# A three-branch encoder layer on one core: operands of the merge stored as parts by the stages that make them, the merge's sums on VectorE, and its weights split one token group earlier

## The chip, the core and the metric

The kernel runs on one core of a Trainium2 chip. The metric is the device time of one execution in microseconds (us). Three executions of the kernel before took 2923.69, 2925.81 and 2926.0 us; the median is 2925.81. The core has five engines with one instruction stream each: TensorE (PE in the profile; its weight loads are PEld), VectorE (DVE), ScalarE (ACT), GpSimd (POOL) and SyncE (SP). Here SP issues every DMA. A stream is worked in order, so an instruction that waits holds up all that stands behind it on its engine.

## What is computed

One layer over 2048 prompt tokens and 8 samples of 16 tokens (17 tiles of 128 tokens), model width 1024:

```python
h = rms_norm(x, norm_g[l])
(a_x, a_b, a_c, a_z, g_q, g_f, g_i, g_z, s_q, s_k, s_v, s_z, m_a, m_b, m_c) = split_cols(h @ w_in[l])
o_a = a_b * causal_conv(a_c * a_x) * silu(a_z)             # A: gated convolution
o_b = rms_norm(hgrn_scan(g_q, g_f, g_i)) * silu(g_z)       # B: gated linear recurrence
o_c = stick_breaking_attention(s_q, s_k, s_v) * silu(s_z)  # C: attention
y_a, y_b, y_c = o_a @ wb[:512], o_b @ wb[512:1024], o_c @ wb[1024:]
m = sigmoid(m_a) * y_a + sigmoid(m_b) * y_b + sigmoid(m_c) * y_c
out = x + m @ w_out[l]
```

## The kernel before, in words

**Parts.** A float32 product is made of three products of shorter floats: each operand is split into a high part (ACT casts it) and a low part (DVE subtracts the high part from the source), and high·high, low·high and high·low are summed (`PASS3`). `split` (L172) issues the two instructions.

**Stages.** (1) Three token groups (5, 6 and 6 tiles, two chunks each; `run_jobs`, L1241). A job is one weight block of `w_in`: 128 columns for channel jobs (24 matmuls of 384 tokens a chunk, L683) or 256 for token jobs (L694). In group 0 `wload` (L180) loads a block into a staging tile `wst` (2 buffers), splits it into a tile `w` (3 buffers, 1 MB, both parts), and `wkeep` (L204) stores the parts in DRAM; groups 1 and 2 load the kept parts straight into a `w` tile. A job's weights are loaded one job ahead. (2) The merge (L1308 to L1438): four groups of token tiles; for each, 12 branch jobs (L1368; 4 for each branch x) and 4 output jobs (L1403), the output jobs of a group between the branch jobs of the next. The merge's own weights (12 blocks of `w_branch`, 8 of `w_out`) are split and kept in the first merge group.

**Background.** Generators of other work are advanced by a budget while the main loop is traced: the recurrence, the attention of the samples (traced during group 1), the prompt's attention (during group 2 and the merge). The final order on each engine is made by a scheduler from the order of tracing and the readiness of operands and buffers, so it moves when tiles or waits change.

**Operands of the merge.** The branches store their results to `OX` in float32 (conv L917, recurrence L1092, attention L344, samples L530). `load_o` (L1329) loads four slices of a branch into `ost` (2 buffers), multiplies those of the attention by the gate `SZ` (L1338), and splits them into `oh` and `ol`. A branch job multiplies its product by the gate `GM` on DVE (L1374, L1376); the sum over branches is a POOL instruction (L1377) except in the last group's last branch; after the third branch the sum `mp` is split into `mh` and `ml`, by a list `due` that holds a split back by one token chunk or two.

**Attention.** For each block of keys: scores into `z` (L306, L307), two sigmoids on ACT (`snb` L310, `sp` L312), a scan and a product on DVE (L319, L324), transposes on PE (L291), a copy of them to `aT` on ACT (L292), and the product with the values (L336). `aT` is one buffer.

Of the kernel before, what the change touches and what calls it, by code (L numbers as in the profile page):

```python
# [16 lines left out]
P = 128  # L17
# [81 lines left out]
def trunk(ctx: ExitStack, tc: tile.TileContext, x_prompt, x_sample, cache_conv, state_hgrn, cache_k, cache_v,  # L99
# [55 lines left out]
    OX = dram.tile([3, 4, P, NTOK], F32, name="OX")  # L155
# [20 lines left out]


    kept = {}

    def wload(pieces, key, places=None):  # L180
# [3 lines left out]
        for n, v in enumerate(pieces):  # L184
            a, b = v.shape[1], v.shape[2]
            w = places[n] if places else wp.tile([P, 2, 1024], F32R, tag="w", name="w")
# [17 lines left out]
    def wkeep(out, key):  # L204
        for n, (_, _, w) in enumerate(out):
# [72 lines left out]
    def attn_pair(m0, m1):  # L278
# [14 lines left out]

        for m in range(m0, m1):
            _, _, si, last, b0, b1, e = steps[m]
            load_step(m)
            load_step(m + 1)
            Q1, Q2, Kt, Vt = held[m]
# [66 lines left out]
    def sample_attention():  # L365
# [163 lines left out]
        nc.scalar.copy(ot, tp.rearrange("p (j t) -> p j t", j=4))  # L529
        nc.sync.dma_start(OX[2][:, :, S0].rearrange("j p t -> p j t"), ot)  # L530
# [26 lines left out]
    class Prepare:  # L557
# [35 lines left out]
        def turn(self, i, kk):  # L593
            ci, ti, _ = self.tiles[i]
            if ti == 0 and kk == 0:
                hh = hp.tile([P, KB, 384], F32R, tag="hh", name="hh")
                hl = hp.tile([P, KB, 384], F32R, tag="hl", name="hl")
                self.hT[ci] = (hh, hl, len(self.group[ci]) * P)
# [242 lines left out]
    class Conv:  # L841
# [67 lines left out]
        def az(self, ci, acc):  # L909
# [7 lines left out]
            nc.sync.dma_start(OX[0, self.j][:, cols(chunk)], y)  # L917
# [39 lines left out]
    def recurrence(g, h, f, k, q, gz, v):  # L957
# [4 lines left out]
        for unit in units:  # L962
# [129 lines left out]
            nc.sync.dma_start(OX[1, h][:, (first + unit[0]) * P:(first + unit[0]) * P + n], ob[:, :n])  # L1092
            yield 0.5

# [145 lines left out]

    def run_jobs(g, jobs):  # L1241
# [5 lines left out]
        def weights(i):  # L1247
            if i < n and i not in ws:
# [5 lines left out]
                 + [(n - 2, 0), (n - 1, 0), (n - 2, 1), (n - 1, 1)])  # L1254
        for at_, (i, ci) in enumerate(order):
            weights(i)
# [52 lines left out]
    wb = w_branch[0]  # L1309
    wo = w_out[0]  # L1310
    GMAX = max(sum(len(c) for c in pg) for pg in PGROUPS) * P

    def branch_w(x, dp):
        return ([wb[x * 512:(x + 1) * 512, dp * 256:(dp + 1) * 256].rearrange("(k p) m -> p k m", p=P)],
                ("branch", x, dp))

    def out_w(s):
        v = wo[:, s * 256:(s + 1) * 256].rearrange("(k p) m -> p k m", p=P)
# [149 lines left out]
```

## Time and profile before

| | |
|---|---|
| median of three runs | 2925.81 us |
| the profiled execution | 2919.97 us, span 2918.1 us |
| PE busy | 2873.3 us (98%) |
| DVE, ACT, POOL busy | 1530.7, 1024.7, 427.9 us |
| moved by DMA | 597.82 MB, mean 205 GB/s |

Busy time is time in which an engine executes; its idle time is put down to what released it at last. The span begins with the first instruction and ends with the last. In the profile of before the first token group ends near 600 us, the second near 1346 us and the third near 2184 us; the merge takes the rest. "PEclk" is the granted share of TensorE's 2.4 GHz.

### The profile page before, as it was taken

How to read it: one execution, taken by the hardware profiler on the slowest of the kernel's cores; microseconds unless marked ns; L12 is line 12 of the kernel's file. 1: busy time of each engine (PE TensorE's matmuls, PEld its weight loads, DVE VectorE, ACT ScalarE, POOL GpSimd, SP SyncE). 2: the span in 40 equal slices, each digit the busy share in tenths (PEclk: the TensorE clock that was granted, in tenths of full speed). 3: DMA queues.
4: the chain of work that ended last, by engine and by line, in shares of the span. 5: the costliest groups of instructions: out<-in, count | busy, mean ns of one | idle time of the engine just before them, and what ended most of it. 6: DMA issues, size and time to landing. Idle time of an engine off the chain costs nothing.

```text
span 2918.1 us, 51343 instructions
## 1 busy us (share of the span) xinstructions
PE 2873.3 (98%) x19511; PEld 2672.2 (92%) x19511; DVE 1530.7 (52%) x3182; ACT 1024.7 (35%) x2359; POOL 427.9 (15%) x859
## 2 busy tenths in 40 slices
PE   9999999999999999999999999999999899999999
PEld 9999999999999999999999999999988787687888
DVE  5454644641252423345434747265577876867643
ACT  4333223242222222114333443334444554444420
POOL 3200000120100000002231111101012412313210
PEclk9999999999999999999999999999999999999999
DMA  8977677767556564436764444434347776677666
GB/s 305 315 257 236 223 227 237 239 229 250 182 184 204 168 213 147 150 128 195 237 200 154 140 151 134 152 121 150 126 155 252 258 268 219 224 251 227 222 230 233
DMA packets 329224, 597.82 MB, mean 205 GB/s; under 512 B 29097, under 2 KB 231170, under 8 KB 291090
## 3 DMA queue, kind: packets, MB, share of 16 engines
q1 hardware_dynamic: 328978, 594.54, 61.8%
q8 instruction: 155, 2.54, 0.4%
q14 instruction: 91, 0.75, 0.1%
HBM read 410.62 MB, written 183.80 MB: 204 GB/s over the span
## 4 chain that ended last, share of the span: by engine, by line
PE 87%; DVE 4%; DMA 4%; issue 3%; POOL 2%; ACT 1%; SPq 0%; DVEq 0%; POOLq 0%; ACTq 0%
PE acc L683 45%; PE acc L694 13%; PE acc L1403 6%; PE acc L1368 4%; PE pv L336 4%; PE tp L291 3%; PE z L1013 2%; PE z L307 2%; PE z L306 2%; DVE pr L319 1%; PE tp L434 1%; POOL mp L1377 1%; DMA w<-W 1%; PE pv L498 1%; DMA gate<-GM 1%
## 5 line engine op out<-in xcount | busy, mean ns | idle before, releaser
L683 PE MATMUL acc<-hh,w 128*128 128x384 f32 (+1 forms) x5376 | 1465.0, 338 | 0.0
L683 PEld LDWEIGHTS acc<-hh,w 128*128 128x128 f32 x5376 | 964.3, 188 | 23.6 <-issue 17.9
L683 PE MATMUL acc<-hl,w 128*128 128x384 f32 (+1 forms) x2688 | 882.5, 328 | 0.0
L683 PEld LDWEIGHTS acc<-hl,w 128*128 128x128 f32 x2688 | 507.1, 189 | 4.9 <-issue 1.0
L694 PE MATMUL acc<-w,hh 128*128 128x256 f32 x2176 | 413.1, 286 | 1.5 <-DMA w<-W 1.2
L694 PEld LDWEIGHTS acc<-w,hh 128*128 128x128 f32 x2176 | 341.8, 188 | 4.0 <-DMA w<-W 1.5
L319 DVE TENSOR_TENSOR_SCAN pr<-snb,carry 128x513 f32<-128x513 f32 x192 | 250.6, 1306 | 117.1 <-ACT snb L310 115.6
L694 PE MATMUL acc<-w,hl 128*128 128x256 f32 x1088 | 306.8, 282 | 0.7 <-DVE hl L175 0.7
L1368 PE MATMUL acc<-oh,w 128*128 128x512 f32 (+2 forms) x960 | 295.4, 368 | 4.2 <-DMA w<-W 1.8
L292 ACT COPY aT<-tp 128x512 f32<-128x512 f32 (+2 forms) x320 | 167.6, 525 | 289.7 <-PE tp L291 289.4
L324 DVE TENSOR_TENSOR sp<-sp,pr 128x512 f32<-128x512 f32 (+2 forms) x320 | 210.3, 657 | 33.7 <-POOL sp L315 7.8
L310 ACT ACTIVATE snb<-z 128x512 f32<-128x512 f32 (+2 forms) x320 | 172.5, 539 | 129.2 <-PE z L307 120.3
L1368 PEld LDWEIGHTS acc<-oh,w 128*128 128x128 f32 x960 | 176.3, 190 | 36.9 <-DVE gate L1376 5.1
L694 PEld LDWEIGHTS acc<-w,hl 128*128 128x128 f32 x1088 | 205.1, 189 | 1.8 <-DVE hl L175 1.3
L319 DVE TENSOR_TENSOR_SCAN pr<-snb,one 128x129 f32<-128x129 f32 (+3 forms) x128 | 114.7, 896 | 163.1 <-POOL snb L315 162.9
L1403 PE MATMUL acc<-w,mh 128*128 128x256 f32 x960 | 189.1, 285 | 2.5 <-DMA w<-W 2.3
L291 PE MATMUL tp<-idf,sp 128*128 128x128 f32 x1088 | 172.0, 273 | 8.1 <-ACT aT L292 7.2
L175 DVE TENSOR_TENSOR w<-wst,w 128x1024 fp32r<-128x1024 f32 x92 | 114.9, 1249 | 121.6 <-ACT w L174 121.1
L1368 PE MATMUL acc<-ol,w 128*128 128x512 f32 (+1 forms) x480 | 174.1, 363 | 3.2 <-DVE ol L175 3.1
L312 ACT ACTIVATE sp<-z 128x512 f32<-128x512 f32 (+2 forms) x320 | 171.3, 535 | 12.6 <-DMA OX<-ot 7.5
L1403 PEld LDWEIGHTS acc<-w,mh 128*128 128x128 f32 x960 | 153.7, 188 | 10.6 <-issue 5.2
L1146 ACT ACTIVATE gm<-acc 128x384 f32<-128x384 f32 (+1 forms) x144 | 68.3, 474 | 260.8 <-PE acc L683 223.0
(296 smaller groups left out, 3730.9 us busy)
## 6 DMA issues: line engine op xcount, KB each, us to landing
w<-W SPq DMA_DIRECT2D x200, 1024.0 KB, 5.3
W<-w SPq DMA_DIRECT2D x92, 1024.0 KB, 5.0
wst<-in_w_in_dram SPq DMA_DIRECT2D x72, 512.0 KB, 6.3
GM<-gm SPq DMA_DIRECT2D x120, 192.0 KB, 2.7
Kt<-KT SPq DMA_DIRECT2D x160, 128.0 KB, 3.6
gate<-GM SPq DMA_DIRECT2D x72, 256.0 KB, 3.1
vc<-in_cache_v_dram SPq DMA_DIRECT2D x64, 256.0 KB, 3.8
kc<-in_cache_k_dram SPq DMA_DIRECT2D x64, 256.0 KB, 3.5
```

The source lines that it names most:

```text
L175: return first, (eng or nc.vector).tensor_tensor(lo, src, hi.bitcast(F32), ALU.subtract)
L291: nc.tensor.transpose(tp[:, j * P:(j + 1) * P], sp[:, j * P:(j + 1) * P], idf)
L292: nc.scalar.copy(aT[:, e, 0:nb, i * P:(i + 1) * P], tp[:, :w].rearrange("p (b q) -> p b q", q=P))
L310: nc.scalar.activation(sn[:, 512 - w:512], z[:, :w], AF.Sigmoid, scale=-0.125)
L312: nc.scalar.activation(sp[:, :w], z[:, :w], AF.Sigmoid, scale=0.125)
L319: nc.vector.tensor_tensor_scan(pr[:, 512 - w:513][:, ::-1], s_in, s_in, one if diag else carry[e][i], ALU.mult, ALU.bypass)
L324: nc.vector.tensor_tensor(sp[:, :w], sp[:, :w], pr[:, 513 - w:513], ALU.mult)
L336: nc.tensor.matmul(pv[64 * e:64 * e + 64, c0:n], Vt[:, j, e], aT[:, e, j, c0:n], start=first and j == 0, stop=last and j == nb - 1, skip_g ...
L683: nc.tensor.matmul(acc[:, :n], w[0][a][:, k], hT[b][:, k, :n], start=k == 0 and i == 0, stop=k == KB - 1 and i == 2)
L694: nc.tensor.matmul(acc[:, :256], hT[b][:, k, ti * P:(ti + 1) * P], w[k // 4][a][:, k % 4], start=k == 0 and i == 0, stop=k == KB - 1 and i ...
L1368: nc.tensor.matmul(acc[:, :n], w[0][a][:, k, dd * P:(dd + 1) * P], box[x][b][:, k, sl], start=k == 0 and i == 0, stop=k == 3 and i == 2)
L1403: nc.tensor.matmul(acc[:, :256], box["l" if b else "h"][:, k, ti * P:(ti + 1) * P], w[k // 4][a][:, k % 4], start=k == 0 and i == 0, stop= ...
```

## The change

- The three stages store both parts: `OX` has a dimension of 2, and `store_parts` splits a result where it is made and stores two tiles. The attention and the samples load `SZ` there and multiply on DVE before the split. `load_o` then only loads eight slices into one tile `o`.
- The sums `mp` are all on DVE, and their split follows at once; `due` is gone.
- The merge's weights are split and stored in group 1: at the second chunk of a channel job, after the ninth place of the order, one of 20 pieces is loaded, split and kept (`split_merge_weights`). The merge loads parts only.
- Every fourth load of kept parts goes to the two staging buffers `wst`, as two DMAs of 0.5 MB, instead of to a `w` tile. The last jobs' places in `oh` and `ol` are gone.
- `hh` and `hl` become one tile `hx` of the same size. The first branch of the next merge group is loaded at an earlier job.

```diff
+    def store_parts(dst, where, x, room):
+        split(room.bitcast(F32R), x.bitcast(F32R), x)
+        for v, part in enumerate((room, x)):
+            nc.sync.dma_start(dst[v][:, where].bitcast(F32), part)
...
+            if (key, n) in kept:
+                turns[0] += 1
+                if turns[0] % 4 == 0:
+                    hl = []
+                    for i in range(2):
+                        x = wp.tile([P, a, b], F32, tag="wst", name="wst", bufs=2)
+                        nc.sync.dma_start(x, kept[key, n][:, i].rearrange("p (a b) -> p a b", a=a).bitcast(F32))
+                        hl.append(x.bitcast(F32R))
+                    out.append((*hl, None))
+                    continue
+            w = wp.tile([P, 2, 1024], F32R, tag="w", name="w")
...
         def store():
-            t = at.tile([P, 512], F32, tag="sp", name="ot", bufs=4)
-            nc.scalar.copy(t[:, :n], box[0][:, :n])
-            nc.sync.dma_start(OX[2, pair][:, q0:q0 + n], t[:, :n])
+            t = gate[0]
+            nc.vector.tensor_tensor(t[:, :n], box[0][:, :n], t[:, :n], ALU.mult)
+            th = at.tile([P, 512], F32, tag="oth", name="oth", bufs=1)
+            store_parts(OX[2, pair], slice(q0, q0 + n), t[:, :n], th[:, :n])
...
+    def split_merge_weights():
+        for pieces, key in [branch_w(x, dp) for x in range(3) for dp in range(4)] + [out_w(s) for s in range(4)]:
+            for n, v in enumerate(pieces):
+                wkeep(wload([v], key, n), key, n)
+                yield
...
+            if ci and len(jobs[i][0][0]) == 1 and at_ > 8:
+                next(extra, None)
             weights(i)
...
-            oh = p3.tile([P, 4, GMAX], F32R, tag="oh", name="oh", bufs=2)
-            ol = p3.tile([P, 4, GMAX], F32R, tag="ol", name="ol", bufs=2)
+            o = p3.tile([P, 2, 4, GMAX], F32R, tag="o", name="o", bufs=2)
             for j in range(4):
-                st = p3.tile([P, GMAX], F32, tag="ost", name="ost", bufs=2)
-                nc.sync.dma_start(st[:, :ntok], OX[x, j][:, gcols])
...
-                split(oh[:, j, :ntok], ol[:, j, :ntok], st[:, :ntok])
+                for v in range(2):
+                    nc.sync.dma_start(o[:, v, j, :ntok].bitcast(F32), OX[x, j, v][:, gcols].bitcast(F32))
...
-                            (nc.vector if final and x == 2 else nc.gpsimd).tensor_tensor(
-                                m, m, gate[:, sl], ALU.add)
+                            nc.vector.tensor_tensor(m, m, gate[:, sl], ALU.add)
                         if x == 2:
-                            box["due"].append((box["h"][:, d, sl], box["l"][:, d, sl], m))
-                            while len(box["due"]) > (0 if final or d == 7 and chunk is pg[-1] else len(pg)):
-                                split(*box["due"].pop(0))
+                            split(box["h"][:, d, sl], box["l"][:, d, sl], m)
```

**What it moves.** First, SP in group 1, kernel before: the loads (L189) of the kept parts of three consecutive jobs (`W31`, `W32`, `W40`), among the gates' stores (GM) and the samples' keys and values (`kc`, `vc`).

```order
L189 DMA w_10549<-W31_3251 128x2048
L1147 DMA GM_77<-gm_10408 128x384
L431 DMA kc_10653<-in_cache_k_dram 128x512
L431 DMA kc_10679<-in_cache_k_dram 128x512
L1147 DMA GM_77<-gm_10481 128x384
L431 DMA kc_10813<-in_cache_k_dram 128x512
L189 DMA w_10670<-W32_3314 128x2048
```

The same place after: `wst_10814` and `wst_10921` stage two pieces of `w_out`; `W85`, `W86` are the stores of their parts; L208 loads kept parts.

```order
L211 DMA wst_10814<-in_w_out_dram 128x4x256
L211 DMA wst_10921<-in_w_out_dram 128x4x256
L529 DMA OCS_78<-od_10960 16x64
L208 DMA w_10870<-W32_3330 128x2048
L227 DMA W85_10818<-w_10813 128x2048
L227 DMA W86_10925<-w_10920 128x2048
L529 DMA OCS_78<-od_10960 16x64 x6
L1175 DMA GM_77<-gm_10989 128x384
L208 DMA w_10992<-W40_4034 128x2048
```

The load of `W32` now stands behind two staging loads, and that of `W40` behind the stores of two split pieces.

Second, PE at the same job, before: the last matmuls with the parts of `W31` (`w_10549`) and the first with those of `W32` (`w_10670`), with sample attention some matmuls earlier (L498, L452, L456).

```order
L498 MATMUL pv_10309<-vc_10715,at__10709 32x128 x4
L452 MATMUL z_10739<-kt_10652,qz_6938 32x256 x4
L456 MATMUL z_10739<-knew_6946,qz_6938 32x16 x4
L683 MATMUL acc_10720<-hh_6911,w_10549 128x384
L683 MATMUL acc_10720<-hl_6912,w_10549 128x384
L683 MATMUL acc_10720<-hh_6911,w_10549 128x384 x2
L683 MATMUL acc_10720<-hl_6912,w_10549 128x384
L683 MATMUL acc_10720<-hh_6911,w_10549 128x384
L683 MATMUL acc_10787<-hh_6735,w_10670 128x384
```

After: `W31` came into the staging pair (`wst_10736`, `wst_10738`), and `w_10870` holds `W32`.

```order
L710 MATMUL acc_10927<-hx_6980,wst_10738 128x384
L458 MATMUL tp_11022<-idf_79,kc_11020 128x128 x4
L458 MATMUL tp_11053<-idf_79,kc_11051 128x128 x4
L458 MATMUL tp_11073<-idf_79,kc_11071 128x128 x4
L499 MATMUL tp_11103<-idf_79,sps0_7050 128x128 x3
L476 MATMUL z_11149<-kt_11019,qz_7006 32x384
L522 MATMUL pv_11150<-vc_11109,at__11107 32x128 x4
L522 MATMUL pv_11150<-vc_11111,at__11107 32x128 x4
L522 MATMUL pv_11150<-vnew_7054,at__11107 32x128 x4
L476 MATMUL z_11149<-kt_11019,qz_7006 32x384 x3
L710 MATMUL acc_10994<-hx_6801,w_10870 128x384 x24
```

Sample attention now stands in one piece between the last matmul with the staging pair and the first with `W32`.

Third, ACT in the merge (first group's third branch), before: casts of `mh`, of operands (`oh`) and of a weight (`w`) among the attention's copies and sigmoids.

```order
L174 CAST mh_25870<-mp_24773 128x384
L174 CAST w_26413<-wst_26414 128x1024
L174 CAST oh_26423<-ost_26425 128x512
L174 CAST mh_25870<-mp_24773 128x256
L292 COPY aT_25939<-tp_26256 128x4x128
L310 ACTIVATE snb2_15009<-z_26262 128x512
L312 ACTIVATE sp_26266<-z_26262 128x512
L174 CAST oh_26423<-ost_26429 128x512
L292 COPY aT_25939<-tp_26288 128x4x128
```

After, at the same chunk:

```order
L175 CAST mh_26269<-mp_25233 128x256
L311 COPY aT_26342<-tp_26613 128x4x128
L333 ACTIVATE snb1_15326<-z_26619 128x512
L335 ACTIVATE sp_26623<-z_26619 128x512
L175 CAST mh_26269<-mp_25233 128x384
L311 COPY aT_26342<-tp_26660 128x4x128
```

The casts of operands and weights are gone from between the copies to `aT`; those of `mh` stay.

## Rows read from the trace of the kernel before

**Rows 1.** Windows: second token group, and merge; columns as its first line says
```profile
core 0: us, PE busy (x) PEld busy (x) DVE busy (x) ACT busy (x) POOL busy (x), PEclk, DMA share, GB/s
600.00:1346.00 746.00, 742.96 (x5521) 720.96 (x5520) 263.72 (x752) 193.26 (x507) 46.89 (x95) 1.00 0.56 183
...
2184.00:2918.00 734.00, 703.58 (x4315) 586.26 (x4314) 495.56 (x640) 305.61 (x596) 172.51 (x266) 1.00 0.72 239
```

**Rows 2.** Waits of PE in the merge: us in total, times, longest
```profile
PE pv L336 <- ACT aT L292: 7.5, 5, 2.7
PE tp L291 <- ACT aT L292: 7.2, 6, 3.3
PE acc L1368 <- DVE ol L175: 3.1, 2, 1.9
PE z L306 <- ACT sp L312: 2.4, 4, 1.4
PE acc L1403 <- DMA w<-W: 2.3, 2, 1.4
```

**Rows 3.** Waits of ACT in the merge
```profile
ACT mh L174 <- POOL mp L1377: 58.1, 28, 5.6
...
ACT oh L174 <- DVE ost L1338: 40.2, 12, 7.4
ACT oh L174 <- DMA ost<-OX: 24.0, 12, 4.0
```

**Rows 4.** Timeline of ACT, 2678 to 2687 us: start, us, engine, line
```profile
2683.26 0.62 ACT L174 CAST mh<-mp 128x512 fp32r<-128x512 f32 x1 [4.17 <-POOL mp L1377]
2685.53 0.62 ACT L174 CAST oh<-ost 128x512 fp32r<-128x512 f32 x1 [1.65 <-DMA ost<-OX]
```

**Rows 5.** Timeline of PE, 2683 to 2687 us
```profile
2686.69 0.55 PE L291 MATMUL tp<-idf,sp 128*128 128x128 f32 x3 [3.25 <-ACT aT L292]
```

**Rows 6.** Groups by line in the merge: count, busy us, mean ns, idle before
```profile
L1377 POOL TENSOR_TENSOR mp<-mp,gate 128x512 f32<-128x512 f32 (+1 forms) x72 | 108.3, 1508 | 144.7 <-DVE gate L1376 132.0 <-issue 12.2 <-DMA gate<-GM 0.3
...
L175 DVE TENSOR_TENSOR w<-wst,w 128x1024 fp32r<-128x1024 f32 x17 | 23.1, 1359 | 7.1 <-ACT w L174 7.1
...
L174 ACT CAST w<-wst 128x1024 fp32r<-128x1024 f32 x17 | 17.9, 1054 | 13.2 <-DMA wst<-in_w_branch_dram 9.1 <-DMA Vt<-VV 2.5 <-PE acc L1403 1.3
...
L1377 DVE TENSOR_TENSOR mp<-mp,gate 128x512 f32<-128x512 f32 x8 | 6.0, 755 | 0.2
```

**Rows 7.** Windows: a stretch in which PE idled in the merge, and the next
```profile
2682.50:2686.50 4.00, 0.94 (x5) 0.59 (x4) 2.29 (x3) 1.59 (x3) 0.73 (x1) 1.00 0.89 207
2686.50:2692.00 5.50, 5.31 (x20) 4.37 (x21) 3.59 (x8) 3.41 (x10) 3.13 (x7) 0.69 0.50 151
```

**Rows 8.** Longest wait of PE in the second group, 600 to 1346 us
```profile
PE acc L694 <- DMA w<-W: 1.2, 1, 1.2
```

**Rows 9.** Loads of kept parts, by tile, 600 to 1345 us
```profile
L189 SPq DMA_DIRECT2D w<-W x71: 319/327/451, 609.3 to 1330.7; - x71
...
DMA to landing us min/median/max: 4.8/5.3/8.4
```

**Rows 10.** DMA issues on the page: count, KB each, median us to landing
```profile
W<-w SPq DMA_DIRECT2D x92, 1024.0 KB, 5.0
...
wst<-in_w_branch_dram SPq DMA_DIRECT2D x12, 512.0 KB, 6.2
```

**Rows 11.** Timeline of PE in the second group, 610 to 640 us
```profile
611.25 0.34 PE L683 MATMUL acc<-hl,w 128*128 128x384 f32 x1
...
611.78 0.34 PE L683 MATMUL acc<-hl,w 128*128 128x384 f32 x1
...
626.98 0.64 PE L498 MATMUL pv<-vc,at__7166 128*32 128x128 f32 x16
...
627.66 0.83 PE L452 MATMUL z<-kt,qz 128*32 128x384 f32 x8
...
637.82 0.60 PE L434 MATMUL tp<-idf,kc 128*128 128x128 f32 x4
```

More of the change, by code (lines that the diff above doesn't have):

```diff
@@ L175, in split, with wload @@
         return first, (eng or nc.vector).tensor_tensor(lo, src, hi.bitcast(F32), ALU.subtract)
+    def store_parts(dst, where, x, room):
+        split(room.bitcast(F32R), x.bitcast(F32R), x)
+        for v, part in enumerate((room, x)):
+            nc.sync.dma_start(dst[v][:, where].bitcast(F32), part)
     kept = {}
-    def wload(pieces, key, places=None):
+    turns = [0]
+    def wload(pieces, key, first=0):
         out = []
-        for n, v in enumerate(pieces):
+        for n, v in enumerate(pieces, first):
             a, b = v.shape[1], v.shape[2]
-            w = places[n] if places else wp.tile([P, 2, 1024], F32R, tag="w", name="w")
+            if (key, n) in kept:
[9 more added lines that the diff above has]
+            w = wp.tile([P, 2, 1024], F32R, tag="w", name="w")
             hi, lo = (w[:, i].rearrange("p (a b) -> p a b", a=a) for i in range(2))
@@ L202, in trunk, with wkeep @@
     rstd_at = [None]
-    def wkeep(out, key):
-        for n, (_, _, w) in enumerate(out):
+    def wkeep(out, key, first=0):
+        for n, (_, _, w) in enumerate(out, first):
             if (key, n) not in kept:
@@ L297, in attn_pair @@
             load_step(m + 1)
+            if m == m1 - 1:
+                gate.append(at.tile([P, 512], F32, tag="ot", name="ot", bufs=1))
+                nc.sync.dma_start(gate[0][:, :n], SZ[pair][:, q0:q0 + n])
             Q1, Q2, Kt, Vt = held[m]
@@ L528, in sample_attention @@
         ot = sa.tile([P, 4, P], F32, tag="cst", name="oct", bufs=3)
-        nc.scalar.copy(ot, tp.rearrange("p (j t) -> p j t", j=4))
-        nc.sync.dma_start(OX[2][:, :, S0].rearrange("j p t -> p j t"), ot)
+        nc.sync.dma_start(ot, SZ[:, :, S0].rearrange("j p t -> p j t"))
+        nc.vector.tensor_tensor(ot, tp.rearrange("p (j t) -> p j t", j=4), ot, ALU.mult)
+        oh = sa.tile([P, 4, P], F32, tag="cst", name="och", bufs=3)
+        split(oh.bitcast(F32R), ot.bitcast(F32R), ot)
+        for v, part in enumerate((oh, ot)):
+            nc.sync.dma_start(OX[2][:, v, :, S0].rearrange("j p t -> p j t").bitcast(F32), part)
         sx.close()
@@ L1091, in recurrence @@
                 nc.vector.scalar_tensor_tensor(ob[:, c], src, hgn, gu[:, c], ALU.mult, ALU.mult)
-            nc.sync.dma_start(OX[1, h][:, (first + unit[0]) * P:(first + unit[0]) * P + n], ob[:, :n])
             yield 0.5
+            oh = hs.tile([P, 2 * P], F32, tag="ktm", name="oh", bufs=1)
+            store_parts(OX[1, h], slice((first + unit[0]) * P, (first + unit[0]) * P + n), ob[:, :n], oh[:, :n])
     def reverse_v(dst, acc):
@@ L1350, in compute @@
                     load_o(2)
+                if dp == 2 and x == 2 and not final:
+                    loads[gi + 1](0)
                 if x == 0 and dp == 0:
@@ L1418, in trunk @@
     tail = []
+    loads = []
     for gi in range(len(PGROUPS)):
@@ L1425, in trunk @@
     alljobs += tail
+    loads[0](0)
     ws = {0: wload(*alljobs[0][0])}
@@ L1428, in trunk @@
         if i + 1 < len(alljobs):
[L1430 to L1435 removed]
+            ws[i + 1] = wload(*alljobs[i + 1][0])
         for cost in compute(ws.pop(i)):
```

43 lines of the change are left out of this document (16 added, 27 removed).

## The prediction

> **What bounds the kernel now.** I read three views in this order: the busy time by stage, the waits of PE, and the waits of the engine that PE waits for. By stage PE is the bound everywhere: in the second token group it is busy 742.96 of 746.00 us, in the merge 703.58 of 734.00 [rows 1]. So an edit can win only the idle of PE, and it can lose wherever it makes PE wait. The idle of the merge is 734.00 − 703.58 = 30.4 us, that of the second group 3.0.
>
> In the merge PE waits mostly for copies to `aT`, 7.5 + 7.2 us, for low parts of operands, 3.1, and for sigmoids, 2.4 [rows 2]. The copies are short; ACT comes late to them, since it waits in order before: 58.1 us for sums on POOL, 40.2 and 24.0 for operands that are to be cast [rows 3]. One place shows it whole: ACT waits 4.17 us for `mp`, casts, waits 1.65 for a load, casts again [rows 4], and only then copies what PE needs; PE has been idle for 3.25 us [rows 5]. The attention's single `aT` gives PE no way round.
>
> In the second group the longest wait of PE is 1.2 us, for kept weights [rows 8]. These are loaded a job ahead into one of three buffers, so a load that takes 4.8 to 8.4 us to land [rows 9] is hidden behind a chunk or two of matmuls. Three matmuls of 384 tokens take 0.53 us (from 611.25 to 611.78, one with `hl` and two with `hh`, [rows 11]); a chunk of 24 takes 4.2 and a job of two 8.5.
>
> **The change, part by part.**
>
> *Operands as parts.* The merge loses 48 pairs of cast and subtraction and the gate's products, and with them the 40.2 + 24.0 us that ACT waits for operands. The stages gain as many splits, in groups where DVE is busy 263.72 of 746.00 us and ACT 193.26 [rows 1], beside matmuls that do not read their results: I cost these at nothing. If that cover went, a split would cost what its two instructions take, about a microsecond. The first operands of the merge are now eight transfers instead of four and their casts; I leave the start of the merge as it was, and keep 3 us either way for the range.
>
> *Sums on DVE.* 72 sums leave POOL, where one takes 1508 ns, and go to DVE at 755 [rows 6]. That adds 72 × 0.755 = 54 us to DVE, which loses more than that in subtractions of operands and weights (17 of 1359 ns for the weights alone). ACT's wait of 58.1 us becomes a wait for DVE: the cast of `mh` stands right behind a product and a sum, and both can stand behind a scan. I take a third of the wait to remain.
>
> Together: of 30.4 us of idle I let 20 go, nearly the 7.5 + 7.2 + 3.1 + 2.4 = 20.2 us of [rows 2]. Upper bound: 26, if the waits for weights, 2.3, and some of the short ones go too (the merge's loads get a fourth place) and little comes anew. Lower bound: 10, if DVE's queue holds `mh` about as long as POOL did. Value: −20.
>
> *The merge's weights in the second group.* This is the part with a price. 20 pieces, each a staging load, a cast of 1054 ns, a subtraction of 1359 [rows 6] and a store of 5.0 us [rows 10], pass through the same three `w` tiles and two staging tiles that the jobs' own weights need; every fourth kept load takes both staging tiles for a whole job. While it holds them, no piece can be staged; the pieces wait for its end, and the next kept load waits in turn on SP behind them. The order shows it: `w_10870` (`W32`) is issued after two staging loads that wait for the last matmul with the staging pair, and is wanted by PE a few short matmuls later. Before, the load of that block stood many rows, a whole job, ahead of its use.
>
> Price of that place, from the last matmul with the pair. SP issues four DMAs at 327 ns [rows 9], 1.3 us; the load lands 5.3 us later (4.8 to 8.4). Two staging loads, themselves 6.2 us to land [rows 10], are ahead of it on the same DMA engines, so I take 7 for the landing: 8.3 us. PE meanwhile has 12 transposes of keys (3 × 0.60), three of `sps` (three quarters of 0.60), four scores (0.83) and 12 products with values (24 records at 0.64 for 16, 0.96) [rows 11], 4.0 us together. It idles 8.3 − 4.0 = 4.3 us; at the landing's ends 2.1 to 5.7.
>
> I count six such places in the order of SP: `W15`, `W27`, `W23`, `W28`, `W32`, `W35`. In the other five the load stands behind a store or a load that waits for a result of PE from just before (a store of `QT`, of `OX`, of a token output; loads of `kc` and `vc`), with 2 to 5 us of PE's work between by the same rows. I take 2 for `W15`, where more work lies between, and 4 for the rest: 2 + 5 × 4 = 22.
>
> In four of them two pieces are staged at once, and the load after the next (`W24`, `W29`, `W40`, `W36`) gets the buffer of a piece: staging 6.2, cast 1.05, subtraction 1.36, store 5.0, load 5.3, and some 1.5 of issues, 20.4 us; PE has 4.0 + 4.3 + 8.5 = 16.8 until then. That is up to 3.6 each; since cast and store may come sooner, 1.5 each: 6. Together +28. Bounds: +9 (six times 1.5, all landings at 4.8 and the next loads in time) and +45 (six times 5.7 and four times 2.7).
>
> *The clock.* After the idle place of [rows 5] the granted clock of the next 5.5 us is 0.69 on average, between the two levels of 1.2 and 2.4 GHz: PE was busy only 0.94 of the 4.00 us before [rows 7]. That costs 5.5 × (1 − 0.69) = 1.7 us. Two such drops stand in the merge; I let both go, −3.4. In the second group six waits of some 4 us, each with matmuls around it, can bring it again: half of them is +5, none 0, all +10.
>
> The Trainium skill (TensorE: Matmul & The Clock Gate, "HAM oscillation — how this bites in real kernels") says that a kernel whose weight slices each end in a wait for a DMA has its clock taken back at each of them, so that every slice starts slow. The place in [rows 7] agrees. By that rule all six drop, and the sum would be 5 us higher, still within the forecast's own range.
>
> *The rest.* The wait of 1.2 us at kept weights [rows 8] goes, since that load gets another place: −1.2. One tile `hx` for two, the later `OX` traffic and the fourth place for weights in the third group I take as nothing, since PE waits for no weight there: no such row stands among its long waits.
>
> Sum: +28 − 20 − 3.4 + 5 − 1.2 = +8.4 us. The profiled execution took 2919.97 us (span 2918.1 and some 2 around it) and would take 2928.4; the median of the three runs shown is 2925.81, so there it is 2934.
>
> **The rivals.**
>
> *The loads land in time (faster).* At the six places the order is only an order: if the chain that stands before a load is done earlier on the chip and 5.3 us of landing are met by sample attention that itself waits for ACT (its copies take over half a microsecond each), PE loses 1.5 us at each place, 9 in all, without a drop of the clock. With the merge's upper bound: +9 − 26 − 3.4 − 1.2 = −21.6, 2904. For it: the only late load of before cost 1.2 us. Against: that one was a job ahead. It decides where the wait at a place stays under 2 us.
>
> *DVE takes POOL's place (slower).* DVE is busy 495.56 of 734.00 us in the merge [rows 1], and now sums stand in its queue ahead of the scans. If ACT waits there as it did for POOL, the merge gains 10 instead of 20 and its clock drops stay: +28 − 10 + 5 − 1.2 = +22, 2948. For it: DVE is the busiest engine after PE. Against: the 24.0 and 40.2 us of operand waits go in any case.
>
> *The chain through the buffers runs over (slower).* If each late load holds SP and what stands behind it (keys, values, the next pieces), the loss goes to its bound: +45 − 20 − 3.4 + 10 − 1.2 = +30, 2956. Against it: after the last piece PE has nothing of the kind to wait for, so it ends by itself.
>
> *Nothing in sum.* The two main terms differ by 8 and each is uncertain by 10; that they cancel to within the bound below is a case of its own, 2926.
>
> **How the numbers follow.** Runs of this kernel differ by about 0.1%; no change means within 0.2%, 5.85 us. The forecast (2932 to 2944) has 0.35; nothing in sum 0.21; the loads in time 0.25; DVE in POOL's place 0.11; the chain that runs over 0.08. Faster is the third, 0.25, and 0.01 of the second: 0.26. Same is the rest of the second and 0.01 of the forecast: 0.21. Slower: 0.53. The range reaches from within the case of faster loads, 2912, to within the longest chain, 2952; the forecast's own is 2928 to 2944.
>
> **What would show it.** Right: waits of PE for kept weights in the second group, some five or six of 2 to 6 us, all between 700 and 980 us, and PE's idle there near 30; idle of the merge near 10; no wait of ACT for POOL or for operands; no drop of the clock in the merge. Wrong: few or no waits for `W` in the second group (then the first rival), or rows in the merge where ACT waits for the DVE sums by tens of microseconds and PE for `aT` as before (then the second). If PE waits in the third group or in the first, a part that I cost at nothing was not free.

## The result, and the profile after

The changed kernel takes 2935.98 us (median of 5 runs, 2933.43 to 2942.11) against 2924.93 for the kernel before (median of 5): 11 us or 0.43% more, ratio 1.0043 with a 95% interval of 1.0030 to 1.0055. The forecast was 2934. The profiled execution has a span of 2934.2 us, 16.1 more than the span of before.

To compare stages I cut both traces at the same matmuls: the last one of each token group's channel jobs. In the kernel before these ends lie at 613.9, 1364.0 and 2179.8 us, after at 616.2, 1418.2 and 2233.6; they replace the rough bounds of [rows 1]. So, by the unrounded ends, the first group is 2.3 us longer, the second 51.9, the third 0.5 shorter, and the merge 37.6 shorter: the net of 16 is a difference of two large numbers. The rows below are windows between these bounds, the second group and the merge, with the columns of [rows 1]; first before, then after.

```profile
614.00:1364.00 750.00, 745.13 (x5518) 722.91 (x5517) 269.94 (x763) 194.23 (x514) 52.48 (x106) 1.00 0.56 184
2180.00:2918.00 738.00, 707.16 (x4336) 588.66 (x4334) 499.39 (x644) 309.61 (x603) 172.69 (x267) 1.00 0.72 239
```

```profile
616.00:1418.00 802.00, 766.10 (x5518) 733.78 (x5517) 301.01 (x805) 220.38 (x554) 52.16 (x106) 0.98 0.65 217
2234.00:2934.00 700.00, 692.57 (x4335) 584.18 (x4333) 457.92 (x646) 267.64 (x537) 57.81 (x195) 1.00 0.77 254
```

In the second group PE does the same 5518 matmuls. Its idle goes from 4.9 to 35.9 us, and its busy time grows by 21.0, of which up to 15.4 is the clock (below). In the merge the idle falls from 30.8 to 7.4, and the busy time falls by 14.6 for the same matmuls (4336 and 4335), of which the clock explains 1.7. A part of the rest I read so: a matmul that stands alone counts its full length, and in a stream the lengths overlap, so each restart after a wait hides some loss in the busy column. PE is interrupted 34 times in the merge before and 5 times after. An estimate: six matmuls take 1.33 us together (at 956.08 below) where one lasts 0.345 us in mean by the page, so in a stream each adds 0.20 us and a restart hides some 0.15; 29 restarts fewer are some 4 us. What the other 8 to 9 us of busy time are, no run shows.

The waits of PE in the second group and then in the merge, after; these answer to [rows 8] and [rows 2].

```profile
PE acc L710 <- DMA w<-W: 8.6, 3, 4.1
PE z L1040 <- DVE WL L1035: 6.6, 2, 5.8
PE hg L827 <- DVE kt L176: 5.2, 4, 3.3
PE tp L458 <- DMA kc<-in_cache_k_dram: 3.4, 2, 2.6
PE tp L458 <- ACT kt L459: 2.3, 3, 1.8
```

```profile
PE acc L1402 <- DMA o<-OX: 2.1, 1, 2.1
PE tp L310 <- ACT aT L311: 1.6, 1, 1.6
```

In the merge the waits for `aT` fall from 14.7 us to 1.6. In the second group only 8.6 us are put down to kept weights; the rest carries the names of small steps of the recurrence and of sample attention. One place shows the plain case. PE first, then SP (start, duration, engine, line):

```profile
956.08 1.33 PE L710 MATMUL acc<-hx,wst 128*128 128x384 f32 x6
957.25 1.03 PE L458 MATMUL tp<-idf,kc 128*128 128x128 f32 x8
...
961.31 0.50 PE L476 MATMUL z<-kt,qz 128*32 128x384 f32 x3
965.89 10.15 PE L710 MATMUL acc<-hx,w 128*128 128x384 f32 x48 [4.08 <-DMA w<-W]
977.80 2.52 PE L710 MATMUL acc<-hx,w 128*128 128x384 f32 x13 [1.76 <-DMA w<-W]
```

```profile
957.26 0.93 SPq L211 DMA_DIRECT2D wst<-in_w_out_dram  x2
958.25 0.49 SPq L529 DMA_DIRECT2D OCS<-od  x1
958.79 0.56 SPq L208 DMA_DIRECT2D w<-W  x1
964.31 2.37 SPq L227 DMA_DIRECT2D W<-w  x2
...
972.42 0.34 SPq L208 DMA_DIRECT2D w<-W  x1
```

The last matmul with the staging pair ends at 957.4; two staging loads and a store go out at once, then the kept load at 958.79, which PE can use 7.1 us later, at 965.89. PE has run out of attention at 961.8 and idles 4.08 us. The load after it (972.42) waits until a piece's store has landed and gives its buffer free, and stands behind the two stores of split pieces (964.31) and six of sample results; it costs 1.76 more.

The other names often hide the same thing. At 859 us PE is said to wait 5.76 us for a step of DVE. But the kept load that its next job needs was issued at 851.29 and took 7.7 us (the page's row for that one load), so it landed at 859.0, and PE starts the job at 859.35. The step was late too, on an engine where it stood behind two split pieces and a scan; had it come sooner, PE would still have waited for the load until 859.0. PE, then SP with the landing, then DVE:

```profile
852.71 0.46 PE L1040 MATMUL z<-WR,WL 128*128 128x128 f32 x2
858.93 0.77 PE L1040 MATMUL z<-WR,WL 128*128 128x128 f32 x2 [5.76 <-DVE WL L1035]
859.35 2.91 PE L710 MATMUL acc<-hx,w 128*128 128x384 f32 x8
```

```profile
851.29 0.42 SPq L208 DMA_DIRECT2D w<-W  x1
...
w<-W SPq DMA_DIRECT2D x1, 1024.0 KB, 7.7
```

```profile
854.04 1.23 DVE L176 TENSOR_TENSOR w<-wst,w 128x1024 fp32r<-128x1024 f32 x1 [1.48 <-ACT w L175]
855.18 1.01 DVE L489 TENSOR_TENSOR_SCAN pr<-sns,pr 128x385 f32<-128x385 f32 x1
856.11 0.27 DVE L1036 TENSOR_TENSOR X<-X,hgf 128x128 f32<-128x128 f32 x1
856.29 1.22 DVE L176 TENSOR_TENSOR w<-wst,w 128x1024 fp32r<-128x1024 f32 x1
```

There are six places where PE idles before such a job, and five have a clock drop. By the semaphore events of the trace the six loads land at 729.97, 768.87, 858.96, 912.88, 965.84 and 1017.81 us, 5.0 to 8.2 us after their issue, and PE starts the jobs at 731.39, 768.92, 859.35, 913.52, 965.89 and 1017.86. So at four places PE starts within 0.4 us of the landing. At the first and the fourth the load had landed 1.4 and 0.6 us before: there small steps of attention and of the recurrence came last, and casts and subtractions of pieces stood before some of them on ACT and DVE (a cast at 723.99 before a copy of keys at 725.70). Windows of the six (columns of [rows 1]; the length minus PE's busy time is its idle):

```profile
720.00:735.00 15.00, 12.25 (x97) 9.03 (x96) 4.29 (x5) 5.56 (x11) 0.00 (x0) 0.77 0.94 349
755.00:772.00 17.00, 11.86 (x100) 9.68 (x99) 7.25 (x16) 6.05 (x15) 2.40 (x4) 0.87 0.73 235
838.00:862.00 24.00, 17.83 (x123) 15.86 (x120) 14.88 (x44) 7.38 (x16) 0.22 (x1) 0.88 0.65 230
905.00:930.00 25.00, 21.84 (x155) 19.24 (x155) 14.23 (x40) 9.04 (x18) 1.12 (x2) 1.00 0.96 344
945.00:982.00 37.00, 29.70 (x219) 26.78 (x218) 5.59 (x7) 10.52 (x20) 0.00 (x0) 0.95 0.83 286
995.00:1020.00 25.00, 17.79 (x145) 15.10 (x144) 6.61 (x10) 10.95 (x25) 0.22 (x1) 0.94 0.82 297
```

The idle is 2.8, 5.1, 6.2, 3.2, 7.3 and 7.2, together 31.8 of the group's 35.9 us. Some drops run past their window: in windows of 10 us at the drops the granted clock is 0.66 four times and, at 966 us, once 0.83, which is 3.4 us each and 1.7, 15.4 in all. That is an upper count, since PE idled for 5.5 of the 30.7 us at the lower clock.

### The profile page after: what moved, and what is told of

Its sections match the earlier page's. It is cut to its first block, busy times and chain, and to the rows that moved or that the text cites. A ratio compares the mean times of both kernels' runs of the same rounds, so it can differ in the third digit from the quotient of the medians.

```text
span 2934.2 us, 51591 instructions
## 1 busy us (share of the span) xinstructions
PE 2881.6 (98%) x19511; PEld 2680.0 (91%) x19511; DVE 1545.4 (53%) x3284; ACT 1022.7 (35%) x2371; POOL 314.9 (11%) x787
## 4 chain that ended last, share of the span: by engine, by line
PE 74%; DMA 3%; DVE 3%; issue 1%; ACT 1%; POOL 1%; SPq 0%; DVEq 0%; ACTq 0%; POOLq 0%
PE acc L710 31%; PE acc L1402 10%; PE acc L721 9%; PE acc L1433 7%; PE pv L359 4%; PE tp L310 4%; PE z L330 2%; PE z L329 2%; PE z L1040 1%; PE tp L458 1%; PE pv L522 1%; DMA xt<-in_x_prompt_dram 0%; DMA wst<-in_w_branch_dram 0%; PE z L476 0%; DMA wst<-in_w_out_dram 0%
## 5 line engine op out<-in xcount | busy, mean ns | idle before, releaser
L710 PE MATMUL acc<-hx,w 128*128 128x384 f32 (+1 forms) x6816 | 1256.3, 334 | 8.7 <-DMA w<-W 8.6
L710 PEld LDWEIGHTS acc<-hx,w 128*128 128x128 f32 x6816 | 1117.1, 190 | 29.4 <-issue 14.8
L721 PE MATMUL acc<-w,hx 128*128 128x256 f32 x2544 | 328.5, 284 | 1.8 <-DVE hx L176 0.9
L721 PEld LDWEIGHTS acc<-w,hx 128*128 128x128 f32 x2544 | 311.3, 188 | 4.9 <-DVE hx L176 1.7
L710 PE MATMUL acc<-hx,wst 128*128 128x384 f32 x1248 | 249.0, 345 | 1.3 <-DVE hgz L1134 0.8
L1402 PE MATMUL acc<-o,w 128*128 128x512 f32 (+2 forms) x1080 | 235.8, 365 | 2.1 <-DMA o<-OX 2.1
L710 PEld LDWEIGHTS acc<-hx,wst 128*128 128x128 f32 x1248 | 215.3, 188 | 8.4 <-issue 3.7
L1402 PEld LDWEIGHTS acc<-o,w 128*128 128x128 f32 x1080 | 186.1, 189 | 34.4 <-issue 6.0
L310 PEld LDWEIGHTS tp<-idf,sp 128*128 128x128 f32 x1088 | 131.9, 141 | 19.6 <-issue 4.4
L329 PE MATMUL z<-Kt,Q 128*128 128x512 f32 (+2 forms) x320 | 129.3, 404 | 0.3 <-ACT sp L335 0.2
```

The source lines that it names most:

```text
L310: nc.tensor.transpose(tp[:, j * P:(j + 1) * P], sp[:, j * P:(j + 1) * P], idf)
L329: nc.tensor.matmul(z[:, :w], Q1[:, i * P:(i + 1) * P], Kt[:, :w], start=True, stop=False)
L710: nc.tensor.matmul(acc[:, :n], w[0][a][:, k], hT[b][:, k, :n], start=k == 0 and i == 0, stop=k == KB - 1 and i == 2)
L721: nc.tensor.matmul(acc[:, :256], hT[b][:, k, ti * P:(ti + 1) * P], w[k // 4][a][:, k % 4], start=k == 0 and i == 0, stop=k == KB - 1 and i ...
L1402: nc.tensor.matmul(acc[:, :n], w[0][a][:, k, dd * P:(dd + 1) * P], box[x][b][:, k, sl], start=k == 0 and i == 0, stop=k == 3 and i == 2)
```

## The experiments

Lengths are those between the bounds named above, in the one profiled execution of each run; the ratio is to runs of the kernel before on the same chip, with its 95% interval.

| run | second group, us | merge, us | median, us | ratio |
|---|---|---|---|---|
| before | 750.1 | 738.3 | 2924.93 | |
| the change | 802.0 | 700.6 | 2935.98 | 1.0043 [1.0030, 1.0055] |
| a_merge_split | 748.0 | 736.5 | 2917.08 | 0.9972 [0.9961, 0.9982] |
| c_no_fourth_g1 | 761.2 | 699.7 | 2895.06 | 0.9896 [0.9880, 0.9913] |
| b_no_fourth | 760.2 | 705.5 | 2899.54 | 0.9917 [0.9900, 0.9934] |
| d_pool_sums | 800.9 | 721.3 | 2953.30 | 1.0095 [1.0080, 1.0110] |
| e_skip_pair | 750.5 | 700.7 | 2885.06 | 0.9857 [0.9842, 0.9872] |
| f_spread | 751.6 | 700.0 | 2883.34 | 0.9850 [0.9833, 0.9866] |
| g_before_dve_sums | 750.4 | 713.2 | 2893.68 | 0.9886 [0.9871, 0.9901] |
| h_no_parts | 761.3 | 705.4 | 2897.94 | 0.9902 [0.9888, 0.9917] |
| l_own_staging | 754.6 | 701.3 | 2889.03 | 0.9882 [0.9865, 0.9899] |
| i_pool_split | 816.4 | 701.6 | 2953.82 | 1.0101 [1.0084, 1.0118] |
| j_due_kept | 749.7 | 714.1 | 2897.24 | 0.9910 [0.9890, 0.9929] |
| k_merge_split_no_parts | 749.4 | 724.4 | 2904.46 | 0.9933 [0.9916, 0.9950] |

### What costs the second group its 52 us

**The pieces taken out** (a_merge_split):

```diff
-        extra = split_merge_weights() if g == 1 else iter(())
+        extra = iter(())
...
+        wkeep(ws[i], alljobs[i][0][1])
         for cost in compute(ws.pop(i)):
```

> The changed kernel, but the merge's weights are again split in the merge's first group (no pieces in the second token group); everything else of the change stays. Between the same matmuls the second token group took 750 us before and 802 after, the merge 738 and 701. If the pieces cause the whole loss of the second group, it is back at 750 to 752 us here, with no drop of the clock. What the merge then shows divides its gain: if operands as parts and sums on DVE carry it, the merge stays at 701 to 710 and the time is some 2885 to 2895 us; if the splitting of the weights had been what held ACT, the merge is back at 725 or more and the time is 2910 to 2925. Rival for the second group: the splits of the branch results (store_parts) or the fourth place for loads cost it; then it stays 10 us or more above 750 without any piece.

The second group takes 748.0 us, with the fourth load still there. So neither the fourth load nor the splits of the branch results cost it anything by themselves. The merge is back at 736.5; that is taken up below.

**The fourth load taken out, in the second group and everywhere** (c_no_fourth_g1, b_no_fourth):

```diff
-                turns[0] += 1
-                if turns[0] % 4 == 0:
+                turns[0] += stage[0] != 1
+                if stage[0] != 1 and turns[0] % 4 == 0:
...
+        stage[0] = g
```

This is the edit of c_no_fourth_g1, where `stage` is the token group, counted from 0; b_no_fourth replaces the condition by `if False:`.

> The changed kernel, but in the second token group every kept load goes to a w tile; the fourth load goes to the staging pair only in the third group and the merge. My theory (the staging pair is held for a job, pieces and next loads bunch behind it): the second group falls from 802 to 752 to 765 us, the time is 2885 to 2900. Rival 1 (the casts and subtractions of the pieces stand in the queues of ACT and DVE and wait there for staging loads, and small steps that PE needs wait behind them): half of the loss stays, 775 to 785, time 2905 to 2920. Rival 2 (three w tiles are too few for jobs and pieces; the fourth load even helped): no gain or a loss, 800 us or more, time 2935 or more.

> The changed kernel without any load to the staging pair, in no stage. The second group as in the run that switches it off there alone, within 2 us. If the fourth place serves the merge, PE waits there for w again as before (2.3 and 1.8 us in total then) and the merge is 2 to 6 us longer than 701; if it serves nothing, the two runs agree within 2 us in total.

The second group falls to 761.2 and 760.2 us, as my theory had it. Pieces without the fourth load cost 11 us, the fourth load without pieces nothing (748.0), both together 52: it is the meeting of the two. In the merge the fourth place is worth 705.5 − 699.7 = 5.8 us.

**A staging tile of their own for the pieces** (l_own_staging): the fourth load stays.

```diff
-                st = wp.tile([P, a, b], F32, tag="wst", name="wst", bufs=2)
+                st = own[0].tile([P, a, b], F32, name="pst") if own[0] else wp.tile([P, a, b], F32, tag="wst", name="wst", bufs=2)
...
+            own[0] = pw.enter_context(tc.tile_pool(name="pw", bufs=1, side="right"))
```

> The changed kernel with one more staging tile, which only the pieces of the second group use; the fourth load keeps the two old ones. If the held staging pair is what delays pieces and next loads, the second group falls from 802 to 750 to 765 us and the time to 2885 to 2900. If the pieces fail on the three w tiles (the fourth load or not), or on the queue of SP, it stays at 780 or more, 2914 or more.

754.6 us: one tile of half a megabyte takes away 47 of the 52. It is the held staging pair: with the same loads on SP, the same count of `w` tiles and the same work of the pieces, PE's idle in the group is 5.0 us again. One thing differs beside it: the single tile lets pieces be staged one at a time, where the pair lets two; no run tells how much of the 47 that is.

**Pieces only where the pair is free, or in every second channel job** (e_skip_pair with the fourth load, f_spread on top of c_no_fourth_g1):

```diff
-            if ci and len(jobs[i][0][0]) == 1 and at_ > 8:
-                next(extra, None)
             weights(i)
             if g or at_:
                 weights(i + 1)
+            if ci and at_ > 8 and all(x[2] for j in (i, i + 1) for x in ws.get(j, ())):
+                next(extra, None)
```

```diff
-            if ci and len(jobs[i][0][0]) == 1 and at_ > 8:
+            if ci and len(jobs[i][0][0]) == 1 and at_ > 8 and i % 2:
...
```

> The changed kernel with the fourth load in all stages, but a piece is only taken in a second chunk (of any job after the ninth place) when neither this job's weights nor the next job's lie in the staging pair, and after the next job's load is traced. If the clash of pair and pieces is the cause and not the count of buffers (my theory now): second group 750 to 762 us, time 2885 to 2897. If what remained without the fourth load (761 against 750) came from too few w tiles, it is nearer to 750 here, since the pair takes a quarter of the loads: 2883 to 2888. If the pieces' casts and subtractions cost by standing in the queues, it stays at 761 or more.

> The run without the fourth load in the second group (761 us there, 2895 in all), with a piece only in every second channel job, so that the 20 pieces spread over twice as many jobs. If the remaining 11 us come from two pieces or loads meeting in the three w tiles, the group falls to 750 to 755 and the time to 2884 to 2890; if each piece costs a fixed half microsecond wherever it stands, nothing changes (760 to 762, 2893 to 2897).

Both bring the group to that of before (750.5 and 751.6), with all 20 pieces in it. The 11 us that stayed in c_no_fourth_g1 were therefore a clash of consecutive pieces too, not a price per piece; whether they met in the three `w` tiles or on SP is not told apart. Nor does e_skip_pair change one thing alone: a piece is also traced behind the next job's load instead of ahead of it, and may go to any job. These are the fastest kernels of the study, 1.4 and 1.5% under the kernel before and about 1.9% under the change (by the ratios).

```profile
616.00:1367.00 751.00, 746.46 (x5523) 723.37 (x5522) 301.84 (x805) 221.92 (x555) 53.22 (x106) 1.00 0.69 231
2182.00:2883.00 701.00, 693.36 (x4339) 585.01 (x4337) 458.31 (x646) 268.15 (x538) 57.95 (x195) 1.00 0.77 254
```

These are the two stages of e_skip_pair: 4.5 us of idle in the second group, with 805 instructions on DVE as in the change.

**The pieces' splits on POOL** (i_pool_split), to see whether the splits in the queues of ACT and DVE were the cause:

```diff
-                    split(hi, lo, st)
+                    if early[0]:
+                        nc.gpsimd.tensor_copy(hi, st)
+                        nc.gpsimd.tensor_tensor(lo, st, hi.bitcast(F32), ALU.subtract)
+                    else:
+                        split(hi, lo, st)
...
```

> The changed kernel, but the pieces of the second group are cast and subtracted on POOL (busy 52 of 802 us there), so that no instruction of theirs stands on ACT or DVE. If PE's waits for steps of DVE and ACT (about 14 of its 36 us of idle in that group) came from splits that wait in these queues for staging loads, they go with their clock drops: second group 775 to 788, 2909 to 2922. If those steps are late only because the kept loads are late and PE has nothing else to do, the idle just moves to the kept loads: 795 to 812, 2929 to 2946.

816.4 us, above both expectations. PE still waits for the same steps of DVE, and longer, with no split piece before them there. The waits for weights themselves are 10.6 us. PE's waits, and DVE at the place that was at 859:

```profile
PE z L1046 <- DVE WL L1041: 12.2, 6, 7.0
PE acc L716 <- DMA w<-W: 10.6, 5, 4.2
```

```profile
855.36 2.32 DVE L1042 TENSOR_TENSOR X<-X,hgf 128x128 f32<-128x128 f32 x1
857.60 1.78 DVE L495 TENSOR_TENSOR_SCAN pr<-sns,pr 128x385 f32<-128x385 f32 x1
859.31 2.36 DVE L1043 TENSOR_TENSOR hgf<-hgf 128x128 f32<-128x128 f32 x1
```

The run is not clean, since POOL's subtractions slow DVE at these very places (last section). That moving the splits to POOL brings nothing is shown; how much the queue alone costs is not. With l_own_staging, where the same splits stand on ACT and DVE and the group takes 754.6, the queue by itself can explain little; beside late loads it had its part at the two places named above.

### What gives the merge its 38 us

**Sums on POOL again** (d_pool_sums):

```diff
-                            nc.vector.tensor_tensor(m, m, gate[:, sl], ALU.add)
+                            (nc.vector if final and x == 2 else nc.gpsimd).tensor_tensor(
+                                m, m, gate[:, sl], ALU.add)
```

> The changed kernel with the sums over the branches on POOL again, as before (the split still follows at once). If the sums on POOL were what made ACT late for the copies (58.1 us of its waiting before), the merge goes from 701 to 715 to 725 us and the time to 2950 to 2960; if the operands' casts were (40.2 and 24.0 us), the merge stays within 5 us and the time is 2936 to 2941. The second group as in the changed kernel, 802 us, five clock drops.

The merge takes 721.3 us: 20.6 of the 37.6 are the engine of the sums. ACT waits for POOL as before, longer even (58.1 then):

```profile
ACT mh L175 <- POOL mp L1411: 73.3, 29, 5.1
```

**The sums alone, in the kernel before** (g_before_dve_sums; j_due_kept is the first edit without the second):

```diff
-                            (nc.vector if final and x == 2 else nc.gpsimd).tensor_tensor(
+                            nc.vector.tensor_tensor(
                                 m, m, gate[:, sl], ALU.add)
...
-                            box["due"].append((box["h"][:, d, sl], box["l"][:, d, sl], m))
-                            while len(box["due"]) > (0 if final or d == 7 and chunk is pg[-1] else len(pg)):
-                                split(*box["due"].pop(0))
+                            split(box["h"][:, d, sl], box["l"][:, d, sl], m)
```

> The kernel before with one edit: all sums over the branches on DVE, and their split at once. The sums were worth 21 us of the merge in the changed kernel (721 against 701). If they are worth the same alone, the merge goes from 738 to 717 and the time to 2905; if operands and weights that are split in the merge still hold ACT, and DVE is the fuller for the sums, the gain is under 8 us: merge 730 to 740, time 2918 to 2928. The second group as before, 750.

> The kernel before with the sums on DVE alone; their splits stay held back by one chunk or two. Sums and immediate split together took the merge from 738 to 713 us. If the engine of the sums carries it, the merge is 711 to 718 and the time 2892 to 2899; if the immediate split does, 725 to 738 and 2906 to 2925.

713.2 and 714.1 us, 2894 and 2897: one changed word, the engine of an addition, gives 24 to 25 us of the merge, more than I expected of it alone. The immediate split adds nothing that can be told apart. And ACT's waits for operands are still there in g_before_dve_sums:

```profile
ACT mh L174 <- DVE mp L1377: 81.2, 33, 25.4
...
ACT oh L174 <- DVE ost L1338: 30.6, 12, 5.7
ACT oh L174 <- DMA ost<-OX: 21.2, 12, 3.7
```

51.8 of the 64.2 us of waiting for operands remain, and yet the merge has lost two thirds of what the change takes off it: these waits were long and cost little. The merge's window in that run; DVE, now with all sums, is busy 504.23 us:

```profile
2181.00:2894.00 713.00, 697.51 (x4335) 584.54 (x4333) 504.23 (x716) 310.67 (x603) 63.19 (x195) 1.00 0.75 247
```

**Operands as float32 again** (h_no_parts, on top of c_no_fourth_g1: the stages store one tile, the merge loads, gates and splits):

```diff
-                for v in range(2):
-                    nc.sync.dma_start(o[:, v, j, :ntok].bitcast(F32), OX[x, j, v][:, gcols].bitcast(F32))
+                st = p3.tile([P, GMAX], F32, tag="ost", name="ost", bufs=2)
+                nc.sync.dma_start(st[:, :ntok], OX[x, j][:, gcols])
...
+                split(o[:, 0, j, :ntok], o[:, 1, j, :ntok], st[:, :ntok])
```

> The run without the fourth load in the second group, but the branches store float32 again, and the merge loads, gates and splits the operands itself (weights split early and sums on DVE stay). If the operands' casts and their waits (40.2 and 24.0 us of ACT's waiting before) were a main cause, the merge goes from 700 to 715 to 730 us and the time to 2910 to 2922; if the sums and the weights were all of it, the merge is 700 to 706 and the time 2893 to 2900. The first and third groups may get 1 to 3 us shorter, since the splits leave them; if they do not, those splits were hidden.

The merge takes 705.4 us against 699.7: the parts, the largest piece of the edit, are worth 5.7. The second group has 761.3, as with the parts, so their splits are hidden there.

**Weights split in the merge, operands float32** (k_merge_split_no_parts: h_no_parts with the edit of a_merge_split).

> The run that splits the merge's weights in the merge (its merge took 736.5 us), but with float32 operands that the merge splits itself; the fourth load stays in the merge. It stands near the kernel before with sums on DVE (713.2). If the stored parts, whose loads are twice as large, cost the 23 us between them where weights are staged at the same time, the merge is 708 to 716 here and the time 2887 to 2896. If it was the fourth load or the earlier load of the next operands, the merge stays at 730 or more, 2908 or more.

724.4, between the two expectations. Splitting the weights in the merge costs 724.4 − 705.4 = 19 us with float32 operands and 736.5 − 700.6 = 36 with stored parts (a_merge_split against the change). The gains do not add up: taken out of the change one at a time, the early split of the weights is worth 36 us, the sums 20.6, the parts 5.7 and the fourth place 5.8, together 68 against 37.6. The early merge of a_merge_split, then of c_no_fourth_g1, with the share of the DMA engines in the column before the last:

```profile
2187.00:2197.00 10.00, 10.00 (x50) 7.61 (x50) 6.67 (x8) 3.73 (x8) 0.00 (x0) 0.87 1.01 348
2207.00:2217.00 10.00, 10.00 (x65) 9.79 (x64) 4.16 (x6) 2.20 (x4) 0.00 (x0) 1.00 1.02 388
```

```profile
2193.00:2213.00 20.00, 18.52 (x88) 11.17 (x88) 12.98 (x14) 9.51 (x20) 0.55 (x3) 0.91 0.79 277
2213.00:2233.00 20.00, 20.00 (x133) 18.77 (x132) 8.39 (x14) 3.84 (x7) 0.00 (x0) 1.00 0.84 249
```

With pieces staged and stored beside operands of twice the size the DMA engines are full; that this is what costs the 17 us between the two is likely and was not tried by itself. Nor is it settled why the merge of k_merge_split_no_parts is 11 us longer than that of g_before_dve_sums: it has the fourth load in the merge, the earlier operand load, one operand tile for two, and not the last weights' own places.

## Why the prediction was right, and where only its sum was

| term | forecast, us | measured, us |
|---|---|---|
| idle of PE in the second group | +28 − 1.2 | +31.0 |
| clock there | +5 | +15.4 at most |
| busy time there otherwise | none | +5.5 |
| idle of PE in the merge | −20 | −23.3 |
| clock there | −3.4 | −1.7 |
| busy time there otherwise | none | −12.6 |
| first and third group | 0 | +2.3 − 0.5 |
| sum | +8.4 | +16.1 (spans), +11.1 (medians) |

The measured column goes by the exact bounds; what is neither idle nor clock is the remainder of each length (51.9 − 31.0 − 15.4, and 37.6 − 23.3 − 1.7).

**The late loads were right, as a mechanism and in size.** Six places, idle of 2.8 to 7.3 us, where I had 2 + 5 × 4 and four times 1.5; at four of them the load itself came last, at two small steps did. The worked example came out almost as written: 7.1 us from issue to use (forecast 7) and 4.08 of idle (forecast 4.3), the load after next 1.76 (forecast 1.5). The runs confirm the cause: the staging pair held for a job, together with the pieces. What I wrote of the sign to look for, waits for kept weights, was too narrow: PE's order had been filled with small steps up to the landing, so most of the idle carries their names. Two other signs were off a little: the last place lies at 1014 to 1018 us and not before 980, and one clock drop stayed in the merge.

**The clock was mis-sized by up to 10 us.** I took 1.7 us a drop from [rows 7] and half of six places; five dropped, and four of them stayed at 1.2 GHz for twice as long as the place of [rows 7] and lost 3.4. The length of the wait does not tell which: the plain wait of 4.08 us at 966 lost 1.7, and the place at 726 with 2.8 us of idle lost 3.4; I leave that open. The rule that I had weighed against this, of the Trainium skill (TensorE: Matmul & The Clock Gate, "HAM oscillation — how this bites in real kernels"), that every such wait for a DMA brings a drop, was nearer: five places of six.

**The merge gave 14 us more than forecast**, outside my bound of 26 for its idle plus the clock. The failed step is "of 30.4 us of idle I let 20 go": the idle did fall by 23.3, but I took the idle column for all that could be won. Another 12.6 us stood in the busy column; restarts are some 4 of them by the estimate above, and what the rest is stays open.

**The two misses have opposite signs and cancel:** +20.1 in the second group (4.2 idle, 10.4 clock, 5.5 other busy time), −14.2 in the merge. Each stage alone, +52 and −38 against +32 and −23, would have been a poor forecast. That the median came within 2 us of 2934 is luck.

**The merge's gain has another cause than I gave.** I let operands, sums and weights share the 20 us, by ACT's waits of 58.1 and 64.2. By the runs the sums on DVE give 24 to 25 alone, and taken out of the change the early split of the weights costs 36, while the parts give 5.7. Waiting time of ACT did not rank them. Of the wait for sums that I let fall to a third, two thirds remained: while attention ran, the 32 casts of `mh` there waited 58.1 us in all before and 39.1 after. Still it was enough.

**The rivals.** That DVE takes POOL's place is refuted by g_before_dve_sums: DVE busy 504.23 of 713 us, and the merge 25 shorter. That the loads land in time is refuted by the four places where PE waits up to the landing. The chain through the buffers did end by itself, after 1018 us. What I costed at nothing, the splits in the stages, shows in no stage: the first group ends between 614.2 and 616.4 us in all these runs, with the splits (614.2 in a_merge_split) and without (616.2 in k_merge_split_no_parts), so its 2.3 us is not theirs.

## What to carry to other kernels

A buffer that gets a second use can be free on average and still be held at the moment that counts: look at who waits for its release, and whether a load that PE needs is queued behind that waiter; here one more tile, or taking pieces only when the pair was free, turned a loss of 0.4% into a gain of 1.2 or 1.4%. Try each edit of a bundle alone: one word in the kernel before gave two thirds of the merge's gain, and the largest rewrite little. And when PE waits for a small step, look at the landing of the load behind it before the step is blamed.

## What the runs showed of the hardware that was not expected

**POOL and DVE got in each other's way.** In i_pool_split DVE instructions of 128x128 that take 0.29 us (as at 856.11 above, 0.27) took 2.32 and 2.36 beside POOL's subtractions of 2.47 and 2.87 us:

```profile
855.06 2.47 POOL L221 TENSOR_TENSOR w<-wst,w 128x1024 fp32r<-128x1024 f32 x1
857.48 1.09 POOL L220 CAST w<-wst 128x1024 fp32r<-128x1024 f32 x1
858.65 2.87 POOL L221 TENSOR_TENSOR w<-wst,w 128x1024 fp32r<-128x1024 f32 x1
```

The DVE instruction that begins at 855.36 ends at 857.68, 0.15 us after POOL's; the one of 859.31 ends at 861.67, again 0.15 us after. The Trainium skill (SBUF — State Buffer, "Who interferes with whom") says that the two engines share a pair of ports under an exclusive lock, and that a DVE instruction with two SBUF inputs contends with a GpSimd instruction that reads SBUF; these rows agree.

The sums on POOL slowed DVE in the merge too. Two groups of DVE instructions there, in the kernel before and then in g_before_dve_sums: products with both inputs in SBUF, and products of which one input is the accumulator `acc`.

```profile
L324 DVE TENSOR_TENSOR sp<-sp,pr 128x512 f32<-128x512 f32 (+3 forms) x162 | 118.4, 732 | 19.0 <-POOL sp L315 5.0 <-ACT aT L292 0.5 <-ACT oh L174 0.5
L1376 DVE TENSOR_TENSOR gate<-acc,gate 128x512 f32<-128x512 f32 (+1 forms) x80 | 47.6, 599 | 30.1 <-DMA gate<-GM 23.2 <-PE acc L1368 6.8
```

```profile
L324 DVE TENSOR_TENSOR sp<-sp,pr 128x512 f32<-128x512 f32 (+3 forms) x163 | 104.5, 642 | 15.1 <-POOL sp L315 3.1
L1376 DVE TENSOR_TENSOR gate<-acc,gate 128x512 f32<-128x512 f32 (+1 forms) x80 | 47.6, 598 | 27.9 <-DMA gate<-GM 21.6 <-PE acc L1368 6.3
```

The first kind falls from 732 to 642 ns in mean, the second stays; subtractions of operands fall from 877 to 717. How many of the 24 to 25 us come from this, and how many from the sum itself (1508 ns on POOL, 606 on DVE in g_before_dve_sums), no run separates. My sum had taken 755 ns for it from eight sums of the last group.
